# A hybrid attention and MLP layer: the slots in which the bias rows are stored, and the order of x and weights at the start

## The chip, the cores and the metric

The kernel runs on one core of a Trainium2 chip. The metric is the device time of one execution in microseconds (us); the time of a kernel is the median over its runs.

## The reference

One decoder layer on x of 256 tokens by 2048 features, all in float32. One projection `w_in` (2048 x 11776) gives q, k and v of 12 heads of mixer A (dilated windows) and of 8 heads of mixer B (blocks; with 256 tokens it is plain causal attention) and two gates. q and k are normalised per head, and a relative-position bias from a table of 32 buckets is added to the logits.

```python
h = rms_norm(x, g_mix)
proj = h @ w_in                      # q, k, v of A; q, k, v of B; two gates
# A: logits = q k * SCALE + bias_tab[rel_bucket(distance)], masked by window and dilation;
#    three groups of four heads, outputs weighted by their softmax denominators
# B: causal softmax attention with its own columns of the same bias table
mixed = sigmoid(g_a) * (ya @ w_branch_a) + sigmoid(g_b) * (yb @ w_branch_b)
x = x + mixed @ w_out
h2 = rms_norm(x, g_mlp)
x = x + square(relu(h2 @ w_up)) @ w_down
```

## The kernel before

Every product with weights is made of three matmuls: the operands are split into a hi part and a lo part (value less hi), and hi*hi, hi*lo and lo*hi are summed in PSUM. Weights come as a stream through three buffers: a piece is four k-tiles of 512 columns (1 MB, one DMA on SP's queue, line 127), and a **slot** is half of a piece, two k-tiles. For each slot ScalarE copies the raw weights to hi (L138) and VectorE subtracts to get lo (L139); TensorE then runs the slot's 12 matmuls of 128x512 (lines 164 to 166). One chunk of `w_in` is 8 slots and 512 output columns. Chunk 0 to 2 is q of A, 3 to 5 k of A, 6 to 8 v of A (slots 48 to 71), 9 and 10 q of B, 11 and 12 k of B, 13 and 14 v of B, 15 to 22 the gates.

The loop at the end of the kernel writes out the order by hand, slot by slot. In step j come first the split of slot j + 2, in odd steps a weight load for a piece further on (some seven slots ahead), then the DMAs that are put down for that step (`at_dma`), then the work on other engines (`at_post`), then the matmuls of slot j, then small work on TensorE (`at_fill`). Each engine and each DMA queue runs its instructions in that order. The steps named in `EARLY` take their `at_post` work ahead of the split instead.

A q or k chunk that ended in slot j is normalised in steps j + 1 to j + 3, transposed in blocks of 32x32 on VectorE (j + 4), written to DRAM by four DMAs (`scatter`, scr<-tq, step j + 6), read back by one (`gather`, step j + 8) and so comes back transposed: this is the bounce. The gather of a k chunk goes straight to its destination (qkva<-scr); that of a q chunk goes to a tile `st`, and in step j + 11 VectorE multiplies it by the gains (L295). A v chunk is only scaled from PSUM in step j + 1.

The bias: in steps 14 to 20 one matmul and one addition give `T["mask"]`, four copies of the 20 heads' bias rows of 384 values. `bias_store(r)` writes copy r to the DRAM tensor `bias_d`, each row 32 times, with one DMA on SP's queue (L359); all four are needed before the first `load` of `attention` (L373, step 71, four steps ahead of the first heads in step 75), which reads along a diagonal.

At the start x is loaded in eight parts. `x_fill(i)` transposes two k-tiles of part i on TensorE, behind the matmuls of slot i - 2; `x_post(i)` in step i - 1 makes their hi (L148, ScalarE) and lo (L149, VectorE), which slot i multiplies; `x_stat` (steps 1, 3, 5 and 6) takes two sums of squares of x on ScalarE (L230).

Of the kernel before, what the change touches and what calls it, by code (L numbers as in the profile page):

```python
# [31 lines left out]
REP = 4  # L32
CW = 512
WARM = (10, 7)
EARLY = (1,)
KD = D // P


def bias_tables():
    """One-hot rows of the bucket of each distance and the masks of the heads; both follow from shapes."""  # L40
    import numpy as np
    hot = np.zeros((NBUCK, 384), np.float32)
    mask = np.full((NH, 384), NEG, np.float32)
    for m in range(383):
        d = 255 - m
        if d < 0:
            continue
        half = NBUCK // 2
        if d < half:
            b = d  # L50
        else:
            b = half + int(math.log(d / half) / math.log(MAXD / half) * (NBUCK - half) + 1e-9)
            b = min(b, NBUCK - 1)
        hot[b, m] = 1.0
        for h in range(NH):
            if h < NA:
                win, dil = DIL[h // NS]
                ok = d <= win and d % dil == 0
            else:
                ok = True  # L60
            if ok:
                mask[h, m] = 0.0
    return hot, np.tile(mask, (REP, 1))
# [3 lines left out]
def hybrid_block_kernel(ctx: ExitStack, tc: tile.TileContext, x, g_mix, w_in, q_norm_a, k_norm_a,  # L67
# [24 lines left out]
    def on(table, j, fn):  # L92
        table.setdefault(j, []).append(fn)

    # ------------------------------------------------------------------ constants
    ident = cp.tile([P, P], F32, name="ident")
    half = cp.tile([P, 8], F32, name="half")
    grow = cp.tile([16, P], F32, name="grow")
# [7 lines left out]
    rel_t = cp.tile([NBUCK, REP, NH], F32, name="rel_t")  # L106
    bias_d = dp.tile([NH, P, 384], F32, name="bias_d")

    # ------------------------------------------------------------------ the stream of weights
    slots = []  # L110

    def stream(src, k0, nk, c0, main, pieces=None):
        """nk k-tiles of 512 columns from row k0, in pieces of four and slots of two."""
        for a in pieces or range(0, nk, 4):
            ap = src[k0 + a * P:k0 + (a + 4) * P, c0:c0 + CW].rearrange("(k p) c -> p k c", p=P)
            for b in (0, 2):
                slots.append((ap, b, a + b, main))
# [22 lines left out]
        split_t[j] = (hi, lo)  # L140

    def split_tr(dst_hi, dst_lo, src, gain=None):
        """hi and lo parts of a transposed tile in PSUM."""
        if gain is None:
            nc.scalar.copy(dst_hi, src)
            nc.vector.tensor_tensor(dst_lo, src, dst_hi.bitcast(F32), op=ALU.subtract)
        else:
            nc.scalar.activation(dst_hi, src, AF.Copy, scale=gain)  # L148
            nc.vector.scalar_tensor_tensor(dst_lo, src, gain, dst_hi.bitcast(F32), op0=ALU.mult,  # L149
                                           op1=ALU.subtract)  # L150

    def tok_major(banks, actT, k, first, last, hi, lo, between=None):
        """Two k-tiles of a chunk for two token tiles: the three partial products of each.
        With three banks the second token tile is cut in two halves of the columns."""
        parts = [(0, 0, CW), (1, 0, CW)] if len(banks) == 2 else [(0, 0, CW), (1, 0, S), (1, S, CW)]
        order = [(i, kk) for i in range(len(parts)) for kk in range(2)]
        if between:
            order = [(i, kk) for kk in range(2) for i in range(2)]
        for i, (n, kk) in enumerate(order):
            t, a, b = parts[n]  # L160
            o = banks[n][:, 0:b - a]
            s_hi = actT[:, k + kk, 0, t * P:(t + 1) * P]
            s_lo = actT[:, k + kk, 1, t * P:(t + 1) * P]
            nc.tensor.matmul(o, lhsT=s_hi, rhs=hi[:, kk, a:b], start=first and kk == 0, stop=False)  # L164
            nc.tensor.matmul(o, lhsT=s_hi, rhs=lo[:, kk, a:b], start=False, stop=False)  # L165
            nc.tensor.matmul(o, lhsT=s_lo, rhs=hi[:, kk, a:b], start=False, stop=last and kk == 1)  # L166
            if between and i == 1:
                between()

    def tok_chunk(src, k0, nk, c0, actT, ka, done):  # L170
        """src[k0:k0+nk*128, c0:c0+512] against k-tiles ka.. of actT; done(banks, slot) when it has run."""
        st = {}

        def main(j, k, hi, lo):
            if k == 0:
                st["b"] = [bank("acc") for _ in range(2)]
            tok_major(st["b"], actT(), ka + k, k == 0, k + 2 == nk, hi, lo, T.get("mid") if j == 0 else None)
            if k + 2 == nk:
                done(st["b"], j)

        return lambda *p: stream(src, k0, nk, c0, main, p)

    def in_pairs(chunks):
        """The first two chunks side by side: the last piece of the first waits for that of the second."""
        a, b = chunks[:2]
        a(0, 4, 8)
        b(0, 4, 8)
        a(12)
        b(12)
        for f in chunks[2:]:  # L190
            f()

    T = {}

    # ------------------------------------------------------------------ transposes beside TensorE
    def blocks(dst, src):
        """The 32x32 blocks of src [128 (i r), n, 128 (j m)], each transposed: dst [128 (i m), j, n, r]."""
        nc.vector.transpose(dst.rearrange("p j n r -> p n j r"), src.rearrange("p n (j m) -> p n j m", m=32))

    def scatter(scr, src):  # L200
        """src [128 (i m), t, j, n r] to scr [t, j, m, i, n r]."""
        for i in range(4):
            nc.sync.dma_start(out=scr[:, :, :, i].rearrange("t j m f -> m (t j) f"),
                              in_=src[32 * i:32 * i + 32].rearrange("m t j f -> m (t j) f"))

    def gather(dst, scr):
        """dst [128 (j m), t, i n r]."""
        nc.sync.dma_start(out=dst, in_=scr.rearrange("t j m i f -> (j m) t (i f)"))

    # ------------------------------------------------------------------ x, its transposes  # L210
    def x_load(i):
        nc.sync.dma_start(out=T["x"][:, :, i * S:(i + 1) * S],
                          in_=xf[:, i * S:(i + 1) * S].rearrange("(t p) c -> p t c", p=P))
# [23 lines left out]
        nc.gpsimd.tensor_scalar(v, s, 1.0 / D, EPS, op0=ALU.mult, op1=ALU.add)  # L237
        nc.gpsimd.tensor_tensor(rstd, v, half[:, 0:2], op=ALU.pow)

    # ------------------------------------------------------------------ projections  # L240
    def qk_done(kind, nh_off):
        """kind: q or k of branch a or b; nh_off: first head of the chunk."""
        def done(banks, j):
            ssq = sp.tile([P, 2, 4], F32, name="ssq")
            qn = []
# [37 lines left out]
            br, w = kind  # L283
# [4 lines left out]
                gather(st["st"], st["scr"])  # L288

            def gain():  # L290
                """q with its tokens in one run: the stationary operand has one free dimension."""
                a = 0 if br == "a" else 1
                q = dst().rearrange("p t f -> p (t f)").rearrange("p (t n i r) -> p t n i r", t=2, n=4, r=32)
                for t in range(2):
                    nc.vector.tensor_scalar(q[:, t], st["st"][:, t].rearrange("p (i n r) -> p n i r", i=4, r=32),  # L295
                                            gqk[:, a:a + 1], None, op0=ALU.mult)
# [42 lines left out]
            o = T["G"][:, t, c * CW:(c + 1) * CW]  # L339
            nc.scalar.activation(o, o, AF.Sigmoid)  # L340

    # ------------------------------------------------------------------ bias of the heads
    def bias_load():
        T["hot"], T["mask"] = tmp("hot")[:NBUCK, :384], cp.tile([REP * NH, 384], F32, name="brow")
        nc.sync.dma_start(out=T["hot"], in_=hot)
# [8 lines left out]
        nc.vector.tensor_tensor(T["mask"], T["bb"][:REP * NH, :384], T["mask"], op=ALU.add)  # L354

    def bias_store(r):
        """Copies r of the rows, 128 of each row in all: a step of 383 then runs along a diagonal."""
        n = P // REP
        nc.sync.dma_start(out=bias_d[:, r * n:(r + 1) * n],  # L359
                          in_=T["mask"][r * NH:(r + 1) * NH, None, :].to_broadcast([NH, n, 384]))  # L360

    # ------------------------------------------------------------------ attention
    def attention(br, heads, cols, yk, base, joint):
        """heads of branch br (bias columns cols); joint: one softmax over all of them, one output."""
        n = len(heads)
        st = {}

# [78 lines left out]
        on(at_fill, base + 11, f_pv)  # L446
        on(at_post, base + 12, p_out)

    # ------------------------------------------------------------------ branches, merge
    def mix_a(c):  # L450
        def done(banks, j):
            def p():
# [6 lines left out]
        return done  # L459

    def bounce_chunk(src, dst, c, j, gain, steps=(3, 6)):
        """src: two [128, 512] tiles, token-major; k-tiles 4c.. of dst."""
        st = {}

        def blk():
# [58 lines left out]
        nc.vector.tensor_scalar(v, s, 1.0 / D, EPS, op0=ALU.mult, op1=ALU.add)  # L524
        nc.vector.reciprocal(rs2, v)

    # ------------------------------------------------------------------ MLP
    def up_chunk(hf, g):
        """512 columns of w_up: four feature-major blocks of 128."""
        st = {}  # L530
        name = f"h{g // 4}"

# [13 lines left out]
                    on(at_post, j + 1 + i, lambda i=i: post(i))  # L546

        def post(i):
            """Two blocks a step; the copies, the squares and the split in steps of their own."""
            if i < 2:  # L550
                for n in (2 * i, 2 * i + 1):
                    u = tmp("u")
# [38 lines left out]
        for part in range(2):  # L591
            stream(w_down, (hf * 32 + part * 16) * P, 16, c * CW, main_of(part))

    # ------------------------------------------------------------------ the program
    for c in range(23):
        if c < 6:
            done = qk_done("aq" if c < 3 else "ak", 4 * c)
# [25 lines left out]
        for c in range(4):  # L623
            down_chunk(hf, c)

    # loads and tiles of the start
    nc.scalar.dma_start(out=grow[0:16], in_=g_mix.rearrange("(k p) -> k p", p=P))
    make_identity(nc, ident)
    nc.gpsimd.memset(half, -0.5)
# [72 lines left out]
    on(at_fill, 19, bias_fill)  # L702
    on(at_post, 20, bias_post)
    for r in range(REP):
        on(at_dma, 22 + 8 * r, lambda r=r: bias_store(r))

    def new(name, tag, shape, dt):
        def f():
# [79 lines left out]
```

## Time and profile before

| | us |
|---|---|
| median of 3 runs | 1418.28 |
| lowest and highest | 1416.72, 1418.5 |
| profiled execution, first to last instruction (its span) | 1414.8 |
| TensorE busy | 1404.5 (99%) |
| VectorE busy | 811.0 (57%) |
| ScalarE busy | 650.1 (46%) |
| DMA traffic | 300.95 MB, 213 GB/s |

For the profiled execution only the span is on record, without what lies around it. In a profile TensorE is PE, its weight loads PEld, VectorE DVE, ScalarE ACT, GpSimd POOL; SPq is SyncE's DMA queue. L139 is line 139 of the kernel. Times of rows count from the first instruction. A row's bracket gives the idle time of the engine just before it, and what ended it. Busy time hides pace: a matmul's row says when it ran, and only the distance between slots says whether the slots follow each other without loss.

### The profile page before, as it was taken

The numbers are of one execution on the slowest core, as the hardware profiler recorded it, in microseconds if no ns is written. First come the engines' busy times: TensorE is split into PE (matmuls) and PEld (weight loads), VectorE is DVE, ScalarE is ACT, GpSimd is POOL, SyncE is SP. The second block draws the span as 40 slices with busy tenths as digits, with TensorE's granted clock in tenths as the row PEclk, the third lists the DMA queues.
The fourth block names the chain that finished last, engine by engine and source line by source line (L and its number), as shares of the span: only waits on it lengthen the run. The fifth ranks groups of instructions, "written<-read, shape, count | busy, mean of one in ns | idle before, by whom it ended". The sixth has DMA issues, their size and how long they took to land.

```text
span 1414.8 us, 17197 instructions
## 1 busy us (share of the span) xinstructions
PE 1404.5 (99%) x6773; PEld 1180.1 (83%) x6773; DVE 811.0 (57%) x989; ACT 650.1 (46%) x956; POOL 28.6 (2%) x44
## 2 busy tenths in 40 slices
PE   9999999999999999999999999999999999999998
PEld 7877888888888888888888888888888888888888
DVE  5645545766555545775657565544445656554443
ACT  7544445454444464444545444433334545443332
POOL 1101000000000000000000000000000000000000
PEclk9999999999999999999999999999999999999999
DMA  8778966778566656778775566565656656556662
GB/s 274 236 233 255 298 201 205 245 257 281 191 208 215 219 191 198 249 256 276 253 225 180 183 190 193 181 205 181 206 184 189 194 179 184 190 191 207 209 204 94
DMA packets 171128, 300.95 MB, mean 213 GB/s; under 512 B 6936, under 2 KB 37032, under 8 KB 171048
## 3 DMA queue, kind: packets, MB, share of 16 engines
q1 hardware_dynamic: 170856, 299.84, 65.7%
q8 instruction: 53, 0.87, 0.3%
q14 instruction: 27, 0.22, 0.0%
q0 software_dynamic: 160, 0.01, 0.0%
q10 hardware_dynamic: 32, 0.01, 0.0%
HBM read 280.43 MB, written 19.40 MB: 212 GB/s over the span
## 4 chain that ended last, share of the span: by engine, by line
PE 95%; DMA 3%; DVE 1%; SPq 0%; ACT 0%; issue 0%; DVEq 0%; ACTq 0%
PE acc L166 18%; PE acc L165 18%; PE acc L164 18%; PE acc L540 8%; PE fill L540 8%; PE fill L542 4%; PE acc L542 4%; PE fill L165 4%; PE fill L166 4%; PE fill L164 4%; DMA st<-scr 2%; DMA scr<-tq 1%; PE fill L383 1%; PE fill L430 1%; DMA raw<-in_w_in_dram 1%; DVE lo L139 0%
## 5 line engine op out<-in xcount | busy, mean ns | idle before, releaser
L139 DVE TENSOR_TENSOR lo<-raw,hi 128x1024 fp32r<-128x1024 f32 (+1 forms) x498 | 606.0, 1218 | 574.1 <-ACT hi L138 572.8
L138 ACT CAST hi<-raw 128x1024 fp32r<-128x1024 f32 (+1 forms) x498 | 522.1, 1049 | 711.9 <-PE acc L166 422.3
L165 PE MATMUL acc<-lo,xT 128*128 128x512 f32 x736 | 287.5, 391 | 4.2 <-DVE lo L139 4.2
L164 PE MATMUL acc<-hi,xT 128*128 128x512 f32 x736 | 290.2, 394 | 0.0
L166 PE MATMUL acc<-hi,xT 128*128 128x512 f32 x736 | 287.3, 390 | 0.6 <-DVE xT L149 0.6
L540 PE MATMUL acc<-x1T,hi 128*128 128x512 f32 x512 | 181.3, 399 | 0.0
L540 PE MATMUL fill<-x1T,hi 128*128 128x512 f32 x512 | 181.3, 399 | 0.0
L165 PEld LDWEIGHTS acc<-lo,xT 128*128 128x128 f32 x736 | 138.7, 189 | 33.8 <-DVE lo L139 5.4
L166 PEld LDWEIGHTS acc<-hi,xT 128*128 128x128 f32 x736 | 138.6, 188 | 30.2 <-DVE xT L149 1.0
L164 PEld LDWEIGHTS acc<-hi,xT 128*128 128x128 f32 x736 | 138.7, 188 | 28.9 <-issue 0.6
L542 PE MATMUL acc<-x1T,lo 128*128 128x256 f32 x512 | 143.8, 281 | 0.0
L542 PE MATMUL fill<-x1T,lo 128*128 128x256 f32 x512 | 143.8, 281 | 0.0
L540 PEld LDWEIGHTS acc<-x1T,hi 128*128 128x128 f32 x512 | 96.2, 188 | 24.0
L540 PEld LDWEIGHTS fill<-x1T,hi 128*128 128x128 f32 x512 | 96.2, 188 | 24.0
L164 PE MATMUL acc<-hi,h 128*128 128x512 f32 (+1 forms) x288 | 108.7, 377 | 0.0
L166 PE MATMUL acc<-hi,h 128*128 128x512 f32 (+1 forms) x288 | 108.7, 377 | 0.0
L165 PE MATMUL acc<-lo,h 128*128 128x512 f32 (+1 forms) x288 | 108.6, 377 | 0.0
L542 PEld LDWEIGHTS acc<-x1T,lo 128*128 128x128 f32 x512 | 96.7, 189 | 0.0
L542 PEld LDWEIGHTS fill<-x1T,lo 128*128 128x128 f32 x512 | 96.7, 189 | 0.0
L165 PE MATMUL fill<-lo,h 128*128 128x512 f32 (+1 forms) x256 | 96.4, 376 | 0.0
L164 PE MATMUL fill<-hi,h 128*128 128x512 f32 (+1 forms) x256 | 96.3, 376 | 0.0
L166 PE MATMUL fill<-hi,h 128*128 128x512 f32 (+1 forms) x256 | 96.2, 376 | 0.0
(123 smaller groups left out, 1199.6 us busy)
## 6 DMA issues: line engine op xcount, KB each, us to landing
raw<-in_w_in_dram SPq DMA_DIRECT2D x89, 1024.0 KB, 5.8
raw<-in_w_up_dram SPq DMA_DIRECT2D x64, 1024.0 KB, 5.3
raw<-in_w_down_dram SPq DMA_DIRECT2D x64, 1024.0 KB, 5.2
raw<-in_w_out_dram SPq DMA_DIRECT2D x16, 1024.0 KB, 5.4
scr<-tq SPq DMA_DIRECT2D x72, 128.0 KB, 5.2
raw<-in_w_branch_b_dram SPq DMA_DIRECT2D x8, 1024.0 KB, 5.6
st<-scr SPq DMA_DIRECT2D x13, 512.0 KB, 5.3
raw<-in_w_branch_a_dram SPq DMA_DIRECT2D x4, 1024.0 KB, 5.3
```

What stands on the lines that cost most here:

```text
L138: nc.scalar.copy(hi[:, o], t[:, o])
L139: nc.vector.tensor_tensor(lo[:, o], t[:, o], hi[:, o].bitcast(F32), op=ALU.subtract)
L164: nc.tensor.matmul(o, lhsT=s_hi, rhs=hi[:, kk, a:b], start=first and kk == 0, stop=False)
L165: nc.tensor.matmul(o, lhsT=s_hi, rhs=lo[:, kk, a:b], start=False, stop=False)
L166: nc.tensor.matmul(o, lhsT=s_lo, rhs=hi[:, kk, a:b], start=False, stop=last and kk == 1)
L383: nc.tensor.matmul(b[:, P:P + S], lhsT=q[:, 1], rhs=k, start=True, stop=True)
L430: nc.tensor.matmul(st["o"][:, o:o + S], lhsT=v[:, 0, h * HD:(h + 1) * HD], rhs=pt[:, 0:2], start=(g == 0 or not joint), stop=False)
L540: nc.tensor.matmul(b, lhsT=hi[:, kk, n * P:(n + 1) * P], rhs=xk.rearrange("p a q -> p (a q)"), start=(k + kk == 0), stop=False)
L542: nc.tensor.matmul(b[:, S:], lhsT=lo[:, kk, n * P:(n + 1) * P], rhs=xk[:, 0], start=False, stop=(k + kk == KD - 1))
```

## The change

The four stores of the bias rows move from steps 22, 30, 38 and 46 to steps 50, 55, 60 and 65. `EARLY` is widened from step 1 to steps 1 to 6: there `x_post` and `x_stat` are put ahead of the split of the weights of slot j + 2. No instruction is added or removed. The rest of the diff takes away comments and docstrings.

```diff
-EARLY = (1,)
+EARLY = (1, 2, 3, 4, 5, 6)
...
     for r in range(REP):
-        on(at_dma, 22 + 8 * r, lambda r=r: bias_store(r))
+        on(at_dma, 50 + 5 * r, lambda r=r: bias_store(r))
```

The loop that reads `EARLY` (unchanged):

```python
    for j in range(n + 1):
        if j == j_up or j in EARLY:
            for f in at_post.pop(j, []):
                f()
        while done_split < min(n - 1, j + 2):
            done_split += 1
            split(done_split)
        while done_load < min(n // 2 - 1, (done_split + 5) // 2):
            done_load += 1
            load_all(done_load)
        for f in at_dma.get(j, []):
            f()
```

## Rows read from the trace of the kernel before

**Rows 1.** Busy time by stretch (count of instructions), granted TensorE clock, DMA share, GB/s

```profile
75.00:100.00 25.00, 22.42 (x92) 18.08 (x91) 11.84 (x15) 11.21 (x24) 2.39 (x3) 0.93 0.79 247
125.00:175.00 50.00, 50.00 (x222) 41.40 (x221) 27.71 (x28) 25.40 (x52) 4.78 (x6) 1.00 0.91 292
175.00:200.00 25.00, 25.00 (x112) 20.70 (x111) 11.69 (x10) 10.60 (x11) 0.00 (x0) 1.00 0.65 210
```

**Rows 2.** Instructions in order of time (start, us, instruction): TensorE's waits, 94 to 121 us

```profile
94.73 0.50 PE L165 MATMUL acc<-lo,xT 128*128 128x512 f32 x1 [2.58 <-DVE lo L139]
...
120.02 0.50 PE L165 MATMUL acc<-lo,xT 128*128 128x512 f32 x1 [1.64 <-DVE lo L139]
```

**Rows 3.** Instructions in order of time: VectorE's gains of the three q chunks of A

```profile
63.26 0.87 DVE L295 TENSOR_SCALAR qkva<-st,gqk 128x512 f32<-128x512 f32 x2
...
91.47 0.88 DVE L295 TENSOR_SCALAR qkva<-st,gqk 128x512 f32<-128x512 f32 x2 [5.35 <-DMA st<-scr]
...
116.75 0.88 DVE L295 TENSOR_SCALAR qkva<-st,gqk 128x512 f32<-128x512 f32 x2 [4.41 <-DMA st<-scr]
```

**Rows 4.** Instructions in order of time: SP's queue, gathers and the first store

```profile
57.19 0.38 SPq L208 DMA_DIRECT2D st<-scr  x1
...
75.54 0.46 SPq L359 DMA_DIRECT2D bias_d<-brow  x1
...
81.18 0.48 SPq L208 DMA_DIRECT2D st<-scr  x1
```

**Rows 5.** Instructions in order of time: ScalarE's splits of the weights, 86 to 148 us

```profile
86.53 1.05 ACT L138 CAST hi<-raw 128x1024 fp32r<-128x1024 f32 x1 [1.67 <-PE acc L166]
...
104.59 1.05 ACT L138 CAST hi<-raw 128x1024 fp32r<-128x1024 f32 x1 [1.67 <-PE acc L166]
...
118.19 1.04 ACT L138 CAST hi<-raw 128x1024 fp32r<-128x1024 f32 x1 [1.65 <-PE acc L166]
...
125.57 1.05 ACT L138 CAST hi<-raw 128x1024 fp32r<-128x1024 f32 x1 [1.67 <-PE acc L166]
...
140.95 2.00 ACT L138 CAST hi<-raw 128x1024 fp32r<-128x1024 f32 x2 [3.44 <-DMA raw<-in_w_in_dram]
...
147.33 1.05 ACT L138 CAST hi<-raw 128x1024 fp32r<-128x1024 f32 x1 [1.31 <-PE acc L166]
```

**Rows 6.** Busy time by stretch, as rows 1, in stretches of 5 us

```profile
95.00:100.00 5.00, 5.00 (x16) 3.93 (x16) 3.16 (x5) 1.05 (x1) 0.00 (x0) 0.66 0.81 228
160.00:165.00 5.00, 5.00 (x23) 4.14 (x23) 2.85 (x4) 2.00 (x2) 0.00 (x0) 1.00 1.03 385
```

**Rows 7.** Landing of raw weight loads, 120 to 170 us, then 170 to 230

```profile
DMA to landing us min/median/max: 5.5/11.5/13.0
...
DMA to landing us min/median/max: 5.0/5.1/5.1
```

**Rows 8.** Instructions in order of time, all engines, at the start

```profile
13.60 0.60 PE L220 MATMUL fill<-ident,x 128*128 128x128 f32 x4
...
14.36 1.04 ACT L138 CAST hi<-raw 128x1024 fp32r<-128x1024 f32 x1
...
15.74 1.05 ACT L138 CAST hi<-raw 128x1024 fp32r<-128x1024 f32 x1 [0.34 <-DMA raw<-in_w_in_dram]
...
16.69 0.83 ACT L148 ACTIVATE xT<-fill,gT 128x256 fp32r<-128x256 f32 x2
...
16.83 1.23 DVE L139 TENSOR_TENSOR lo<-raw,hi 128x1024 fp32r<-128x1024 f32 x1 [0.17 <-ACT hi L138]
...
17.55 0.40 PE L165 MATMUL acc<-lo,xT 128*128 128x512 f32 x1
...
17.97 0.87 DVE L149 SCALAR_TENSOR_TENSOR xT<-fill,gT,xT 128x256 fp32r<-128x256 f32 x2
...
18.50 0.50 PE L166 MATMUL acc<-hi,xT 128*128 128x512 f32 x1 [0.56 <-DVE xT L149]
...
19.52 0.63 ACT L230 ACTIVATE junk<-x 128x512 f32<-128x512 f32 x1
```

## The prediction

> **What bounds the kernel now.** First the page's busy times: TensorE is busy for nearly the whole span, so a change that leaves its instructions as they are, as this one does, can give back only idle time, or time at a lower clock. Next, the stretches show where that lies near the bias stores: from 75 to 100 us TensorE is busy only 22.42 of 25 us at a granted clock of 0.93, while from 125 to 175 us, with the third and fourth store in it, it is busy 50.00 of 50 [rows 1]. TensorE's own rows name the waits: 2.58 us at 94.73 and 1.64 us at 120.02, both for a lo half of the weights from VectorE [rows 2]. VectorE was late because ahead of that split stands the gain of a q chunk (L295), which sat 5.35 and 4.41 us until the gather st<-scr had landed; the first q chunk's gain, at 63.26, shows no wait [rows 3]. On SP's queue the first store goes out at 75.54 and the gather behind it at 81.18, so that took until about 91.4, over 10 us; the first q chunk's gather went out at 57.19 with no store beside it and had landed by 63.26, in 6.1 us [rows 3, 4]. So two of the four stores hit a gather on which VectorE stands still. The other two hit k chunks, whose gather goes straight to its destination with nobody waiting.
>
> **The price of the two stalls.** ScalarE's splits run one to a slot and are released by TensorE, so they count slots: from 125.57 to 147.33 are 8 slots, 2.72 us each [rows 5]. From the split at 86.53 to that at 104.59 are 5 slots, 13.60 us undisturbed, and took 18.06: 4.46 us lost. From 118.19 to 125.57 are 2 slots, 5.44, and took 7.38: 1.94 us. Together 6.40 us. Of the first, 2.58 is waiting; most of the rest is the clock, which after that wait stood at a mean of 0.66 over 95 to 100 us, so for most of them at 1.2 GHz instead of 2.4, and 16 matmuls show there where undisturbed stretches of 5 us show 23 [rows 6].
>
> **Part 1, the stores leave slots 22, 30, 38, 46.** With nothing else in those slots moved, chunks 1 and 2 are what chunk 0 is: bounce and weights. Their gathers should land in about 6 us instead of 10. Chunk 1's gain was due right after the split ending near 86.1 (91.47 less 5.35), and TensorE was short by 2.58 of the 5.35, so some 2.8 us of lateness are free. A gather out at 81.18 that takes 6.1 lands at 87.3, 1.2 us late, and is covered. For chunk 2 the free part is 4.41 - 1.64 = 2.8, too. Gain: 6.40 us. The bounds: nothing, if the bounce alone makes the gather late, and 6.40. I take 6.40, by chunk 0.
>
> **Part 2, the stores enter slots 50, 55, 60, 65.** Each is 20 x 32 x 384 x 4 bytes, 0.98 MB, on SP's queue, and the mask that it waits for was ready long before, so SP never stands for it. Behind it in the queue: weight loads; behind the store of slot 55 also the gather of the last k chunk (written in slot 53), wanted only in slot 75. Nothing on VectorE waits for a DMA in these slots: v chunks have no bounce. What can suffer is the weights. Without a store loads land in 5.0 to 5.1 us; where the third and fourth store run they need up to 13.0 [rows 7], and that cost TensorE nothing: the latest split, at 140.95, was 1.78 behind its slot (125.57 + 5 x 2.72 = 139.17) [rows 5], and a split comes two slots, 5.44 us, ahead of its matmuls, of which it needs about 2.3 (ScalarE 1.05 and VectorE 1.23 [rows 8]). So 5.44 - 2.3 - 1.78 = 1.4 us were left: loads may take 14.4 us, 9.3 more than 5.1. By bytes: from slot 49 to 67 there are ten loads (10.5 MB), four stores (3.9) and one bounce (1.05), 15.5 MB in 18 slots, 49.0 us, plus those 9.3: no stall if the queue moves 266 GB/s. The stall-free 50 us with two stores moved 292 GB/s, with more bounces in them than these slots have, and 385 at the best [rows 1, 6]. Cost: 0; bounds 0 and about 4.5 (the largest stall seen, 4.46); nothing below zero, since the weights of these slots have no wait to give back. I take 0, by that stretch; the cover is those 9.3 us.
>
> Here a rule speaks against the change. The Trainium skill, page "DMA: Bandwidth & Descriptors", section "Why a DMA increments its semaphore by 16 and not by 1", says that a DMA runs on the largest k up to 16 engines that divides both sides' slowest dimension; a store's is 20, so 10 engines. Its sum would be, as an estimate, 15.5 MB spread as 11.5/16 + 3.9/10 = 1.11 MB on each of the ten, 19.1 GB/s over 58.3 us; 385 GB/s over 16 engines is 24.1. By that rule the queue still keeps pace, with a thinner margin: the sum is the same, and (a) and (b) below have one reason more. No row here counts a transfer's engines.
>
> The attention's first bias load (slot 71) must find all stores landed. The last goes out 6 slots, 16.3 us, before it; the longest landing near a store is 13.0. Cost 0.
>
> **Part 3, x ahead of the weights in slots 2 to 6.** One wait is there to remove: in slot 3 the third matmul starts at 18.50, for the lo half of x (L149), where by the spacing of 0.23 it was due at 17.55 + 0.23 = 17.78: 0.72 us [rows 8]. VectorE reached x at 17.97, behind the split at 16.83, whose raw weights had only come at 15.74. With x first: its transposes were done at 14.2, ScalarE is free of the earlier split at 15.40 and VectorE at about 16.7, so lo of the first tile is there near 17.1, the second near 17.5: in time. The split that is pushed back ends near 18.7, wanted at 20.4. In slots 3, 5 and 6 the squares of x (two of 0.63, 1.3 us) now also stand ahead of the split on ScalarE. Per slot it then has 0.83 + 1.3 + 1.05 = 3.2 us against 2.72 plus about 0.45 of transposes; counted forward, the split for slot 8 ends near 31.3 and is wanted near 32.9. The raw loads that wait for these splits go out some 1.5 us later, with 11 us until their use. Gain 0.72, plus 0.1 for the refilled pipeline: 0.8; bounds 0 and 0.85.
>
> **Sum.** 6.40 + 0.8 - 0 = 7.2 us. The profiled execution spans 1414.8; the median, 1418.28, is 3.5 above it, and I take that distance as fixed: 1407.6 in the span, **1411.1** in the median.
>
> **Rivals.**
> (a) Late weights in the v chunks: if the queue moves 249 GB/s, as little as the first stretch's 247, the 15.5 MB take 62.2 us, 3.9 beyond the 58.3, and with 1.9 of lower clock, as after the first stall, up to 5.8 us: 1411 to 1417. For: five slots between stores instead of eight. Against: 292 [rows 1].
> (b) Slower, by one mechanism: the same backlog at under 227 GB/s. Then 15.5 MB take over 68.3 us, 10 more than the cover, which eats the gain of 7.2 and 2.8 more; at 220 it is 70.5, 12.2 late, with the clock 14.1: 1425. Against: the row of v chunks with weights alone shows 210 at a share of 0.65, so the queue had room [rows 1].
> (c) The change doesn't do what it says: the bounce itself makes the gathers late, and only part 3 pays: 1417.5. Against it is chunk 0.
> (d) The clock's part of the first stall (1.9) is not in every execution, or part 3 gives nothing: 1412 to 1413.
>
> **How the numbers follow.** Forecast 0.60 (1410 to 1412); (d) 0.18; (a) 0.12; (c) 0.04; (b) 0.04; 0.02 for more than counted. The range, 1409.6 to 1414.8, holds the forecast, (d), and the nearer half of (a). A measurement of this kernel tells about 0.2%, 2.8 us, from no change; the line for faster is 1415.4. Forecast, (d), three quarters of (a) and the 0.02 lie under it: 0.89; within: 0.07; slower: 0.04.
>
> **What would show it.** Right: L295 of the second and third q chunk without a wait for st<-scr; TensorE without the waits of 2.58 and 1.64; the clock at 1.00 from 75 to 100 us; no wait of L166 for xT in slot 3; raw loads landing in 7 to 13 us in slots 50 to 67 with TensorE never waiting for lo. Wrong: a wait of TensorE for lo there behind ScalarE waiting for raw (a, b), or L295 still waiting over 2.8 us (c).

## The result and the profile after

| | before | after |
|---|---|---|
| median of 5 runs, us | 1418.28 | 1408.92 |
| lowest to highest | 1416.64 to 1418.95 | 1408.7 to 1409.56 |
| span of the profiled execution | 1414.8 | 1406.9 |
| time of the profiled execution | not on record | 1408.98 |

The ratio is 0.9934 (95% interval 0.9922 to 0.9946): 9.4 us faster, where 7.2 were forecast. 1408.92 lies 0.7 us under the lower end of the range and 2.2 us under the forecast of 1411.1: the direction held and the size did not. Two executions among the experiments below, at 2000.47 us (EARLY alone) and 2857.48 us (the stores alone, second time), were slow and stand in no number of this text.

Busy time by stretch of the kernel after (the stretch; busy time and count of PE, PEld, DVE, ACT, POOL; granted clock; DMA share; GB/s), against [rows 1, 6]:

```profile
75.00:100.00 25.00, 25.00 (x112) 20.68 (x111) 14.02 (x15) 12.80 (x26) 2.39 (x3) 1.00 0.80 252
125.00:175.00 50.00, 50.00 (x222) 41.43 (x221) 28.57 (x28) 23.36 (x41) 4.78 (x6) 1.00 0.83 262
175.00:200.00 25.00, 25.00 (x112) 20.69 (x111) 11.69 (x10) 10.37 (x11) 0.00 (x0) 1.00 0.86 280
95.00:100.00 5.00, 5.00 (x24) 4.13 (x22) 2.16 (x2) 1.99 (x2) 0.00 (x0) 1.00 0.99 308
```

From 75 to 100 us TensorE now runs without a gap at a clock of 1.00, 112 matmuls instead of 92. The stores' traffic shows from 150 us on: the v chunks of 175 to 200 us move 280 GB/s instead of 210, and TensorE is still busy all the time.

VectorE's gains of the three q chunks, in order of time, against [rows 3]:

```profile
62.19 0.88 DVE L295 TENSOR_SCALAR qkva<-st,gqk 128x512 f32<-128x512 f32 x2
...
84.97 0.88 DVE L295 TENSOR_SCALAR qkva<-st,gqk 128x512 f32<-128x512 f32 x2
...
106.73 0.88 DVE L295 TENSOR_SCALAR qkva<-st,gqk 128x512 f32<-128x512 f32 x2
```

None has a bracket: all three gathers had landed. The second is out at 79.94 on SP's queue and there by 84.97, 5.0 us at most where it took 10.3:

```profile
79.94 0.38 SPq L208 DMA_DIRECT2D st<-scr  x1
```

The landing of raw weight loads, first of 40 to 120 us, then of 120 to 200 us, against [rows 7], and ScalarE's one wait for them in the slots that now have the stores:

```profile
DMA to landing us min/median/max: 5.3/5.7/6.9
...
DMA to landing us min/median/max: 4.9/8.4/11.4
```

```profile
180.88 1.05 ACT L138 CAST hi<-raw 128x1024 fp32r<-128x1024 f32 x1 [1.89 <-DMA raw<-in_w_in_dram]
```

The loads' longest landing is 11.4 us, within the 14.4 that the prediction allowed, and no row of TensorE waits there.

At the start, slot 3 on TensorE, against [rows 8]: the third matmul follows the second by 0.24 us and waits for nothing.

```profile
17.32 0.40 PE L165 MATMUL acc<-lo,xT 128*128 128x512 f32 x1
17.56 0.39 PE L166 MATMUL acc<-hi,xT 128*128 128x512 f32 x1
```

Counted by ScalarE's splits slot by slot, the two profiles part in four places: by slot 14 the kernel after is 1.07 us ahead; between the splits of slots 28 and 34 it gains 4.46, between those of slots 34 and 42 1.94, together 6.40; and near slot 231, in the output projection, 0.39. That is 7.86 of the 7.9 us between the spans. The last piece was not forecast and does not belong to the change: there a block transpose on VectorE waits for an earlier scatter, 1.19 us before and 0.77 after, and the wait came out between 0.64 and 1.33 us in the experiments below, whatever they changed (1.24 in a second profile of the changed kernel).

### The profile page after: what moved, and what is told of

It reads as the page before. It is cut to its first block, busy times and chain, and to the rows that moved or that the text cites. A ratio compares the mean times of both kernels' runs of the same rounds, so it can differ in the third digit from the quotient of the medians.

```text
span 1406.9 us, 17199 instructions
## 1 busy us (share of the span) xinstructions
PE 1401.6 (100%) x6773; PEld 1179.3 (84%) x6773; DVE 811.2 (58%) x989; ACT 650.2 (46%) x956; POOL 28.6 (2%) x44
## 2 busy tenths in 40 slices
DMA packets 171128, 300.95 MB, mean 214 GB/s; under 512 B 6936, under 2 KB 37032, under 8 KB 171048
## 4 chain that ended last, share of the span: by engine, by line
PE 99%; DMA 0%; DVE 0%; issue 0%
PE acc L164 20%; PE acc L165 20%; PE acc L166 20%; PE fill L540 9%; PE acc L540 9%; PE acc L542 4%; PE fill L542 4%; PE fill L164 4%; PE fill L165 4%; PE fill L166 4%; PE fill L383 1%; PE fill L430 1%; PE fill L382 0%; PE fill L432 0%; PE fill L220 0%; DMA x<-in_x_dram 0%
```

## Experiments

Each was timed beside the kernel before on its chip; a median is given with that of before there. Time less span is 2.0 to 2.6 us in every execution of every kernel there.

**The kernel before, once more.** No edit.

> The kernel before once more, to see in another execution whether its two stalls have the same size. Theory A (the difference between its executions lies in these two stalls): TensorE waits at the same two places, behind L295, and span less undisturbed slots follows from their sum; all else stands as in the first profile within 0.5 us.

Time 1418.71, span 1416.6, so 2.1 us around the span and not 3.5. TensorE's two waits, against [rows 2], and VectorE's gains, against [rows 3]:

```profile
94.39 0.50 PE L165 MATMUL acc<-lo,xT 128*128 128x512 f32 x1 [2.34 <-DVE lo L139]
...
120.30 0.50 PE L165 MATMUL acc<-lo,xT 128*128 128x512 f32 x1 [3.85 <-DVE lo L139]
```

```profile
91.13 0.88 DVE L295 TENSOR_SCALAR qkva<-st,gqk 128x512 f32<-128x512 f32 x2 [5.11 <-DMA st<-scr]
...
117.03 0.88 DVE L295 TENSOR_SCALAR qkva<-st,gqk 128x512 f32<-128x512 f32 x2 [6.62 <-DMA st<-scr]
```

By the same count of slots the stalls cost 2.63 and 5.75 us here, 8.39 together, 2.0 more than in the first profile; the span is 1.8 longer. The stalls differ from execution to execution, and of the three profiles with the stores in the old slots and the old shape (the third follows under EARLY alone) the first held the smallest. Beside the experiments the kernel before spread over 1415.7 to 1421.6 us; the changed kernel spread over 1.1 us. Theory A holds.

**The stores alone, and EARLY alone.** The changed kernel with one of its two edits undone:

```diff
-EARLY = (1, 2, 3, 4, 5, 6)
+EARLY = (1,)
```

> The stores in slots 50, 55, 60 and 65 as in the changed kernel, EARLY as before. Theory A (the two stalls behind the stores are 6.4 us in the profiled execution, and 1.5 us more in the executions that make the median of the kernel before): median 8 us below the kernel before, near 1410.3, all executions within 1 us of each other, and a span about 6.4 below 1414.8. Theory B (the extra 1.5 us of the median come from the start, part 3): 6.4 us below, near 1411.9, with executions as far apart as those of the kernel before.

1410.1 (before 1416.89), ratio 0.9945 (0.9933 to 0.9957), the lowest and highest 0.8 us apart. 6.8 us where 8 were expected, with a median of the kernel before that was 1.4 lower than on the first chip; the level, 1410.3, was met, and with it theory A.

```diff
-        on(at_dma, 50 + 5 * r, lambda r=r: bias_store(r))
+        on(at_dma, 22 + 8 * r, lambda r=r: bias_store(r))
```

> EARLY as in the changed kernel, the stores in slots 22, 30, 38 and 46 as before. Theory A: only the wait in slot 3 goes, about 1 us: median near 1417.2, and the executions stay on two levels some 1.5 to 2 us apart. Theory B: 2.4 us or more, near 1415.8, and the two levels become one.

1417.47 (before 1416.89), ratio 0.9997 (0.9988 to 1.0006): no gain to be seen. The interval ends at 1.7 us faster, so it rules out theory B's 2.4 us and leaves room for theory A's one microsecond, which it does not show either. In its profile the start is 1.29 us ahead of the first profile of before, as theory A wants, and the two stalls then cost 7.79 instead of 6.40. Part 3's microsecond can't be told from the spread of the stalls here, so its price was sought where there are no stalls: the changed kernel beside the one with the stores alone.

> The changed kernel once more, on one chip with the kernel that has only its stores moved, to give part 3 its own price. Theory A (part 3 is the wait in slot 3 and what jitter the start has, about 1 us; the rest of what the forecast missed is the distance between span and time, about 2.1 us for every kernel and not 3.5): 0.8 to 1.3 us below the kernel with the stores alone, and time less span 2.0 to 2.3 in every execution. Theory B (part 3 is worth 2 us or more in unprofiled executions): 2 us or more below it.

> The stores moved and EARLY as before, beside the changed kernel. Theory A: 0.8 to 1.3 us above the changed kernel, near 1410. Theory B: 2 us or more above it.

1409.36 against 1410.26 (before 1418.13): part 3 is worth 0.9 us once the stores have moved. Theory A holds, with time less span at 2.0 to 2.5 for the one and 2.1 to 2.4 for the other.

**The gain two slots later, the stores where they were.**

```diff
-                on(at_post, j + 11, gain)
+                on(at_post, j + 13, gain)
```

> The kernel before, with the gain of a q chunk (L295) two slots later, in step j + 13 instead of j + 11; stores and EARLY as before. Theory A (the whole price of a store in slots 22 and 30 is VectorE standing at L295 ahead of the weights' split): both stalls of TensorE are gone with the stores where they were, and the median is some 8 us below the kernel before, near 1410.3, as with the stores moved. Rival (the store delays the weights themselves, or the clock falls by itself there): TensorE still waits at one or both places, and the median stays over 1414.

1410.62 (before 1416.89), ratio 0.9948 (0.9935 to 0.9962): the gain of moving the stores, with all four stores left in slots 22 to 46. The gains on VectorE now stand where the gathers have landed:

```profile
92.32 0.88 DVE L295 TENSOR_SCALAR qkva<-st,gqk 128x512 f32<-128x512 f32 x2
114.10 0.88 DVE L295 TENSOR_SCALAR qkva<-st,gqk 128x512 f32<-128x512 f32 x2
```

So the price of a store in the q chunks was VectorE's wait at L295 ahead of the split, and not late weights: ScalarE still waits 2.3 us for raw there, and TensorE never does. Theory A holds.

**The stores crowded.** The changed kernel with

```diff
-        on(at_dma, 50 + 5 * r, lambda r=r: bias_store(r))
+        on(at_dma, 50 + r, lambda r=r: bias_store(r))
```

> The changed kernel with the four stores in slots 50, 51, 52 and 53 instead of 50, 55, 60 and 65: 3.9 MB at once. By the prediction's sum of bytes (8.6 MB of loads, stores and scatter from slot 49 to 55 in 16.3 us and 9.3 us of cover need 337 GB/s, the stretches with stores moved 292): loads land later than 14.4 us, TensorE waits for lo behind raw about 4 us, and with the lower clock after that the median is 4 to 6 us above the changed kernel, near 1414. Rival (the queue has more room than that, or the cover is larger): within 1 us of the changed kernel's 1408.9.

1422.14 (before 1416.89), 13 us above the changed kernel; 4 to 6 were expected. Neither reading holds as put: the queue has less room than the sum of bytes gave it, not more. TensorE's waits:

```profile
180.76 0.80 PE L164 MATMUL acc<-hi,xT 128*128 128x512 f32 x1 [5.64 <-ACT hi L138]
182.02 0.80 PE L165 MATMUL acc<-lo,xT 128*128 128x512 f32 x1 [0.47 <-DVE lo L139]
```

and ScalarE's split, which waited for raw longer than any before it:

```profile
179.66 1.99 ACT L138 CAST hi<-raw 128x1024 fp32r<-128x1024 f32 x2 [11.61 <-DMA raw<-in_w_in_dram]
```

After the first wait these matmuls run 0.80 us each: the granted clock is 0.50 from 178 to 185 us, which is 1.2 GHz. What is odd stands in the 30 us from 148 to 178: with loads overdue the engines moved 219 GB/s at a share of 0.74 (first line below), while the prediction had counted on 292. Three runs ask why. They keep the bytes and, but for a fifth store in the second run, the slots, and change which rows of the mask one DMA reads. In all three the mask's 80 rows are ordered by head and copy (the mask table and the small matmul's operand follow, the latter by one more copy on VectorE). In the first, each DMA takes a quarter of the copies of all 80:

```diff
-        n = P // REP
-        nc.sync.dma_start(out=bias_d[:, r * n:(r + 1) * n],
-                          in_=T["mask"][r * NH:(r + 1) * NH, None, :].to_broadcast([NH, n, 384]))
+        n = P // REP // REP
+        nc.sync.dma_start(out=bias_d.rearrange("h (r n) m -> (h r) n m", r=REP)[:, r * n:(r + 1) * n],
+                          in_=T["mask"][:, None, :].to_broadcast([REP * NH, n, 384]))
```

> The four stores in slots 50 to 53, as in the run that lost 11 us there, with the same bytes and the same number of packets, but each DMA takes a quarter of the copies of all 80 mask rows instead of all copies of 20 rows. Theory C (a store of 20 rows occupies only ten of the DMA engines, so in the dense run the ten were the limit at about 240 GB/s): spread over all engines each carries 246 KB of stores instead of 393, some 6 to 7 us less at 22 GB/s; the stall shrinks to about 4 us, median near 1413, and no stretch between the stores and their landing stays under 250 GB/s while raw loads are overdue. Rival (stores are slow by their packets of 1.5 KB, whatever the rows): the stall stays, median near 1422.

1409.8 (before 1418.13), where theory C said 1413: of the stall one wait of TensorE of 0.7 us is left. In the second, five DMAs of 16 adjacent rows with all 32 copies, in slots 50 to 54:

```diff
-        n = P // REP // REP
-        nc.sync.dma_start(out=bias_d.rearrange("h (r n) m -> (h r) n m", r=REP)[:, r * n:(r + 1) * n],
-                          in_=T["mask"][:, None, :].to_broadcast([REP * NH, n, 384]))
+        n = P // REP
+        nc.sync.dma_start(out=bias_d.rearrange("h (r n) m -> (h r) n m", r=REP)[16 * r:16 * r + 16],
+                          in_=T["mask"][16 * r:16 * r + 16, None, :].to_broadcast([16, n, 384]))
```

> The same bytes as the dense run, now in five stores of 16 mask rows with all 32 copies, in slots 50 to 54. Theory C (what counts is how many DMA engines a store's rows are dealt out to: 20 rows go to ten, 16 and 80 to all sixteen): as with 80 rows, no stall of more than 1 us, median near 1410, although fewer rows are read than in the dense run. Rival (what counts is how many rows, and so partitions, a store reads from: 80 are quick, 20 slow): the stall of the dense run stays or grows, median 1422 or more.

1426.45 (before 1417.9): worse than 20 rows. Theory C alone falls. In the third, 20 rows with all 32 copies again, on every fourth partition (the new lines):

```diff
+        n = P // REP
+        nc.sync.dma_start(out=bias_d[:, r * n:(r + 1) * n],
+                          in_=T["mask"].rearrange("(h r) m -> h r m", r=REP)[:, r:r + 1].to_broadcast([NH, n, 384]))
```

> The dense run once more: four stores in slots 50 to 53, each of 20 rows with all 32 copies, as in the run that lost 13 us against the changed kernel; the only difference is that the 20 rows lie on every fourth partition from 0 to 76 instead of on 20 adjacent ones. Theory D (what makes a store slow is that its rows lie on adjacent partitions, read through few ports): as quick as with 80 rows, median 1410 to 1412. Theory C (20 rows are dealt out to ten DMA engines, wherever they lie): the stall stays, median near 1422. Rival E (32 copies in a row of one partition are slow to read, 8 are not): the stall stays too, with the DMA share near 0.93 at low GB/s as with 16 rows, where theory C leaves it at 0.6 to 0.8.

1416.34 (before 1417.96): between the two, and so none of the three as put. The stretch from 148 to 178 us, one line for each kernel: 20 adjacent rows, 80 rows, 16 adjacent rows, 20 rows spread.

```profile
148.00:178.00 30.00, 27.12 (x120) 22.14 (x118) 12.96 (x13) 8.98 (x9) 2.19 (x2) 0.99 0.74 219
```

```profile
148.00:178.00 30.00, 30.00 (x134) 24.84 (x133) 15.33 (x15) 11.01 (x11) 2.20 (x3) 1.00 0.94 297
```

```profile
148.00:178.00 30.00, 26.82 (x119) 21.89 (x117) 12.97 (x13) 8.88 (x10) 1.95 (x2) 1.00 0.92 214
```

```profile
148.00:178.00 30.00, 27.37 (x121) 22.34 (x119) 12.96 (x13) 9.78 (x10) 2.39 (x3) 1.00 0.77 246
```

Two things can be read apart here. The time that the 16 engines spend on a megabyte is share x 16 x 30 us over the megabytes moved: 54 us with 20 adjacent rows (0.74 x 480 / 6.57), 51 with 80 rows, 69 with 16 adjacent rows, 50 with 20 rows spread. These megabytes are loads as well as stores. The traces also have each packet: the stores' packets of 1536 bytes took a mean of 84 ns with 20 adjacent rows, 69 with 80, 152 with 16 adjacent and 72 with 20 spread. So few adjacent partitions make the packets slow, and spreading the same 20 rows takes that away. The share itself stays at 0.74 and 0.77 with 20 rows, wherever they lie, while loads are overdue, and is 0.92 and 0.94 with 16 and 80: with 20 rows a part of the engines has nothing to do. The pages' counts of DMA packets agree with theory C: 171128 in both runs with 20 rows, 171152 with 80 and 171168 with 16. The 24 and 40 more are packets of 4 bytes, and 24 is 4 x 16 less 4 x 10, 40 is 5 x 16 less 4 x 10: as if each engine that a store runs on added one, sixteen engines with 80 and 16 rows and ten with 20. Theory D is right for the first effect and theory C for the second; both make up the dense run's 13 us. Rival E is out for the first: the spread rows have all 32 copies. For the second, from 20 rows spread to 80, the copies in a row change as well, but 32 copies are read nearly as quickly as 8 (72 ns against 69). What else changes there, the order in which the addresses of `bias_d` are written, was not tested apart.

**80 rows, in the old and in the new slots.** The edit of the 80-row run in the kernel before, then with the new EARLY as well, then in the changed kernel:

> The kernel before, stores in slots 22, 30, 38 and 46, EARLY as before, with each store taken from all 80 mask rows as in the run beside it. Theory C: each store holds the engines some 1.7 us less, the gathers of the q chunks land that much sooner, L295 waits 3 to 4 us instead of 4.4 to 6, of which 2.8 are free: TensorE loses 1 to 2 us in all, median near 1412. Rival: L295 waits as before and the median is that of the kernel before, 1417 to 1418.

1410.68 (before 1418.13), better than theory C's 1412. The gathers are still late, but by little more than what is free:

```profile
88.28 0.88 DVE L295 TENSOR_SCALAR qkva<-st,gqk 128x512 f32<-128x512 f32 x2 [2.13 <-DMA st<-scr]
...
111.02 0.88 DVE L295 TENSOR_SCALAR qkva<-st,gqk 128x512 f32<-128x512 f32 x2 [3.11 <-DMA st<-scr]
```

The loss there is 0.67 us instead of 6.4 to 8.4, where theory C said 1 to 2.

> The stores left in slots 22, 30, 38 and 46 but taken from 80 rows each, with the new EARLY. Theory C: the store's shape is the whole cause, so that moving it is worth no more than what is left of the stall there (0.6 us): median near 1409.7, within 0.2% of the changed kernel. Rival: the places themselves cost 2 us or more, median over 1411.

1409.74 (before 1417.9): 0.4 to 0.8 us above what the changed kernel gave in its two rounds of runs, with the stores never moved. Theory C's number was met; its reason, as shown, is half of it.

> The changed kernel with its stores taken from 80 rows each, in slots 50, 55, 60 and 65. No wait of TensorE is left there in the changed kernel, so nothing can be won: within 0.5 us of the changed kernel, near 1409, and the raw loads land in at most 9 us instead of 11.4.

1409.25 (before 1417.9), and raw landings of up to 10.4 us, not 9. Nothing is won on the changed kernel, since no wait of TensorE was left there. No run beats it by more than the spread of its own runs.

## Why the prediction was wrong, and where it was right

- **Sum, the step that failed.** It took the 3.5 us between the median of before and the span of its profile as fixed time around a span. It is about 2.1 for every kernel (1408.98 less 1406.9 after, 1418.71 less 1416.6 before). The other 1.4 us were a difference between executions: with 2.1 around its span the profiled one took about 1416.9 (an estimate, since its time is not on record), near the lowest of before (1416.64), and its stalls were the smallest of the three profiles that hold them; a change that removes the stalls removes that difference as well. This is 1.4 of the 2.2 us missed.
- **Part 1**, 6.40 us from the slots of the profile: 6.40 between the two profiles, with L295 free of its wait; putting the gain later gave the same gain with the stores in place. Right in mechanism and size, for that execution; in a second one the same two stalls were 8.39 us.
- **Part 2**, nothing: right, with 11.4 us as the longest landing. The reason given was too simple. It priced a store by its bytes at the mean rate of stretches with stores; the crowded run missed by 8 us for that, since a store of 20 adjacent rows slows packets and leaves engines idle. The change stays clear of it because its stores stand five slots apart.
- **The rule in part 2.** The ten engines of the Trainium skill (page "DMA: Bandwidth & Descriptors", section "Why a DMA increments its semaphore by 16 and not by 1") agree with what the runs show with 20 rows (share 0.74 and 0.77 with work waiting, 0.94 with 80). The prediction had no row that counts engines; the counts of DMA packets above fit ten and sixteen. The estimate of 19.1 GB/s for each engine took every packet to be equally quick, and the run with 16 rows shows that they are not.
- **Part 3**, 0.8 us: 1.07 in the profiles, 0.9 between medians without stalls. Of the 1.07, 0.71 is the wait in slot 3 and 0.13 the matmuls behind it, as forecast; 0.23 is there already at slot 3's second matmul (17.55 before, 17.32 after), ahead of the wait. The start differs between executions: counted to slot 14, six profiles with the old EARLY lie 0.58 to 1.31 us behind the changed kernel's first one (mean 0.94), nine with the new EARLY from 0.36 ahead to 0.18 behind (mean 0.12 ahead), 1.07 between the means. With the 0.4 us near slot 231 the 0.27 too little here make up the rest of the miss, but for 0.1.
- **Rivals.** (a) and (b) needed the queue at 249 or 227 GB/s; the stretches of the stores moved 262 and 280 with no wait. Crowded, (a) and (b) came true. (c) is out: the gather without a store beside it lands in 5.0 us at most. (d) looked at the right thing, executions that differ, with the wrong sign: the profile was on the small side.

## What to carry to other kernels

A profile is one execution: when the time lost hangs on a race between transfers, its stalls differ from one execution to the next, and a gain is to be summed against that execution's own time, with the spread of the runs added to the stalls that the change removes. An instruction that waits for a DMA on an engine that also feeds TensorE costs what stands behind it, so it can be moved later as well as the transfer can be moved away. And before a store is given another place, look at its shape: stores of few adjacent rows, each read many times, were nearly the whole cause here (1410.68 us with 80 rows in the old slots).

## What the runs showed of the hardware

At equal bytes, four crowded stores from an 80-row tile cost 13 us in 20 adjacent rows each, 7 in 20 rows on every fourth partition and under 1 in 80 rows; five of 16 adjacent rows cost 17. The engines' time for a megabyte rose from 50 to 69 us with 16 adjacent rows, and with 20 rows a quarter of the engines' time stayed idle while loads were late. Adjacent rows are not equally slow everywhere: a packet of a store of 20 adjacent rows took a mean of 97 ns in the old slots of the kernel before and 75 in the new slots of the changed one; why is open. On the slow packets the Trainium skill, page "SBUF — State Buffer", section "Door 1: The DMA port swizzle", says that a transfer's bandwidth goes by the number of ports that its partitions reach and that neighbouring partitions share a port; the order of the runs agrees, and none of them counts ports. SP's queue feels it too. Its rows in the run with 20 adjacent rows crowded, in order of time:

```profile
158.46 6.01 SPq L127 DMA_DIRECT2D raw<-in_w_in_dram  x1
...
166.93 15.15 SPq L203 DMA_DIRECT2D scr<-tq  x4
```

One weight load took 6.01 us to issue, where the two before it took 0.37 and 0.38, and the four scatters behind the last store 15.15, where they take 2.41 and 2.54 in the q chunks of the changed kernel. With 80 rows in the same slots the same two took 2.28 and 8.69.
